# Output projection and embedding gate as 512-column matmuls with high and low parts side by side

## The chip, the cores and the metric

One Trainium2 chip, one core of it. The program is one launch: two transformer layers over 256 tokens. The metric is device time in microseconds (us), from runs of the same program; lower is better. The profile is one more execution with the hardware profiler on. TensorE is called PE, its weight loads PEld, VectorE DVE, ScalarE ACT, GpSimd POOL, and SyncE, which issues the big DMAs, SP.

## The reference

Two layers of a trunk, width 1024, 256 tokens, 32-bit floats. In each layer the normalised state is projected, three mixers (differential attention "da", a state space mixer "ssd", gated linear attention "gla", 512 channels each) run on the projections, and then come the parts that matter here:

```python
mix = jnp.concatenate([y_da, y_ssd.astype(y_da.dtype), y_gla.astype(y_da.dtype)], axis=-1)
h = h + mix @ w_out[i]
f = rms_norm(h, ffn_norm[i])
h = h + (jax.nn.silu(f @ w_ffn_gate[i]) * (f @ w_ffn_up[i])) @ w_ffn_down[i]
h = h + jax.nn.sigmoid(h @ ple_w_gate[i]) * (p[i] @ ple_w_proj[i])
```

`mix @ w_out` is the output projection (1536 to 1024), `h @ ple_w_gate` the embedding gate (1024 to 1024).

## The kernel before

**Products in three parts.** Every 32-bit operand is split in a high part and a low part, and a product is high x high + high x low + low x high. An activation block is one tile of 128 channels x 512: columns 0 to 255 hold the high part of the 256 tokens, columns 256 to 511 the low part. `product_t` with weights as the stationary operand knows two forms. The narrow one (L242 to L245) issues for each 128-channel step k three matmuls of 256 columns, each with a weight load of its own: high weight x high activation (L243), high weight x low activation (L244), low weight x high activation (L245). The wide one (L235 to L239) issues two: high weight x the whole 512 columns (L237), low weight x the 256 high columns (L239), and takes two k at a time (two L237, then two L239). A narrow result is 128x256 and two blocks of output channels share a PSUM bank; a wide result fills a bank of 512 columns, whose two halves have to be added afterwards. The feed-forward uses the wide form; the output projection and the gate use the narrow one.

**Stages.** The work of a layer is a list of units, one per block of weights: projections with the mixers' steps between them, four units `w_o1` (`first`, the ssd and gla channels of `mix`, 8 steps k), two units `w_o2` (`second`, the da channels, 4 steps k, two pairs of output blocks each), 22 units `w_f`, 16 units `w_d`, four units `w_g` (`gate`). After each unit the weights of the second next are loaded (`load_w`): one DMA of 1 MB into one of 3 stage buffers `st`, then for each half of the unit ACT writes the high part `wh` (L212) and DVE the low part `wl` (L213, which reads `wh`). `wh` and `wl` have 6 buffers each, so an L212 can start only when PE has read the half unit six halves earlier to its end.

**The ends of the stages.** Results of the output projection are added to the state `h` on DVE (L934 in `first`, L943 in `second`). `operand` then makes the next activation block from `h`: ACT the high part (L273), DVE the low part (L274). `square` (ACT L283, POOL L286) sums squares for the norm. The first `w_f` unit is issued with `split=6`: steps k 0 to 5 of both output blocks, then k 6 and 7, the blocks that are made last. The da channels of `mix` come from `parts` (ACT L387, DVE L388), one pair for each of four channel blocks and each of two halves of the tokens; four of them read one PSUM tile `pm`. Between `w_d` and `gate`, DVE L1000 updates `h`, and ACT L269 and DVE L270 make the block.

**Order.** A scheduler places the instructions of all engines at build time from its own estimate of when data is there; each engine then runs its list strictly in that order. There are 5 PSUM banks `acc` for these products, used in turn.

Of the kernel before, what the change touches and what calls it, by code (L numbers as in the profile page):

```python
# [16 lines left out]
ALU = mybir.AluOpType  # L17
# [3 lines left out]
P = 128  # L21
D = 1024
T = 256
# [22 lines left out]
O_FFN = O_ATTN + 8  # L46
# [61 lines left out]
def trunk_kernel(ctx: ExitStack, tc: tile.TileContext, a: dict):  # L108
    nc = tc.nc
    pe, dve, act, pool = nc.tensor, nc.vector, nc.scalar, nc.gpsimd  # L110
# [13 lines left out]
    def slot(s, dt=F32):  # L124
        return sp.tile([P, SLOT], dt, tag="slot", name=nm(s))
# [4 lines left out]
    def bank_acc():  # L130
        return ps.tile([P, 512], F32, tag="acc", bufs=NACC, name=nm("acc"))
# [4 lines left out]
    def v3(ap, n):  # L136
        return ap.rearrange("p (a b) -> p a b", a=n)


    par = [cp.tile([P, NPAR], F32, name=f"par{i}") for i in range(DEPTH)]  # L140
    cst = cp.tile([P, NCST], F32, name="cst")
    pos = cp.tile([P, 2, a["pos"].shape[-1]], I32, name="pos")
    h = cp.tile([P, KD, T], F32, name="h")
# [85 lines left out]
    def product_t(out, w, lo, x, ks, n, wide):  # L229


        if wide:

            pairs = list(zip(ks, w, strict=True))
            for p0 in range(0, len(pairs), 2):  # L235
                for k, (wh, _) in pairs[p0:p0 + 2]:
                    pe.matmul(out, wh[:, lo:lo + P], x[k], start=k == 0, stop=False)  # L237
                for k, (_, wl) in pairs[p0:p0 + 2]:
                    pe.matmul(out[:, :T], wl[:, lo:lo + P], x[k][:, :T], start=False, stop=k == n - 1)  # L239
            return  # L240
        for k, (wh, wl) in zip(ks, w, strict=True):
            sh, sl, hi = wh[:, lo:lo + P], wl[:, lo:lo + P], x[k][:, :T]  # L242
            pe.matmul(out, sh, hi, start=k == 0, stop=False)  # L243
            pe.matmul(out, sh, x[k][:, T:], start=False, stop=False)  # L244
            pe.matmul(out[:, :T], sl, hi, start=False, stop=k == n - 1)  # L245

    def gemm_t(blocks, x, wide=False, split=0, apart=False):


        n = len(x)  # L250
        apart = apart or split or wide
        pbs = [bank_acc() for _ in range(2)] if apart else [bank_acc()]
        outs = [pb if wide else pb[:, :T] for pb in pbs] if apart else [pbs[0][:, :T], pbs[0][:, T:]]
        for k0, k1 in ((0, split), (split, n)) if split else ((0, n),):
            for c in range(2):
                w, lo = blocks(c)
                product_t(outs[c], w[k0:k1], lo, x, range(k0, k1), n, wide)
        return [(outs[c], c, c + 1) for c in range(2)] if apart else [(pbs[0], 0, 2)]
# [5 lines left out]
    def operand(x, c, gains):  # L264

        xc = slot("x", F32R)
        hi, lo = xc[:, :T], xc[:, T:]
        if gains is None:
            act.activation(hi, h[:, c], AF.Copy)  # L269
            dve.tensor_tensor(lo, h[:, c], hi.bitcast(F32), ALU.subtract)  # L270
        else:
            g = gains[:, c:c + 1]
            act.activation(hi, h[:, c], AF.Copy, scale=g)  # L273
            dve.scalar_tensor_tensor(lo, h[:, c], g, hi.bitcast(F32), ALU.mult, ALU.subtract)  # L274
        x.append(xc)

    def both(out, pb):
        act.activation(out, pb[:, T:], AF.Copy)
        dve.tensor_tensor(out, pb[:, :T], out, ALU.add)

    def square(c2, acc):
        sq = slot("ssq") if acc is None else slot("sq")
        act.activation(sq, h[:, 2 * c2:2 * c2 + 2].rearrange("p a b -> p (a b)"), AF.Square)  # L283
        if acc is None:
            return sq
        pool.tensor_tensor(acc, acc, sq, ALU.add)  # L286
        return acc
# [514 lines left out]
    def step(S, *names):  # L802
        for n in names:
            if n not in S["gens"]:
                S["gens"][n] = {"da": da_gen, "ssd": ssd_gen, "gates": gla_gates_gen, "gla": gla_gen}[n](S["i"], S)
            next(S["gens"][n], None)
# [119 lines left out]
    def out_units(i, S, x):  # L926

        def first(c2):
            def go(w):
                if c2 < 4:  # L930
                    step(S, *PLAN_OUT[c2])
                pb = gemm_t(lambda c: (w, c * P), S["mix"][1] + S["mix"][2])[0][0]
                hv = h[:, 2 * c2:2 * c2 + 2]
                dve.tensor_tensor(hv, v3(pb, 2), hv, ALU.add)  # L934
            return go

        def second(c4):
            def go(w):
                for c2 in (2 * c4, 2 * c4 + 1):
                    for pb, lo, hi in gemm_t(lambda c: (w, (2 * (c2 % 2) + c) * P), S["mix"][0],  # L940
                                             apart=c2 == 3):
                        hv = h[:, 2 * c2 + lo:2 * c2 + hi]
                        dve.tensor_tensor(hv, v3(pb, hi - lo), hv, ALU.add)  # L943
                        for c in range(2 * c2 + lo, 2 * c2 + hi):
                            operand(x, c, par[i][:, O_FFN:O_FFN + 8])
                    S["acc"] = square(c2, S["acc"])
            return go

        for c2 in range(4):
            units.append((a["w_o1"][i, c2], KD, T, first(c2)))  # L950
        for c4 in range(2):
            units.append((a["w_o2"][i, c4], 4, 512, second(c4)))

    def ffn_units(i, S, x, xg):
# [3 lines left out]
        def summed(pieces):  # L958
            gu = slot("gu")
            for pb, c, _ in pieces:  # L960
                both(gu[:, c * T:(c + 1) * T], pb)
            return gu
# [27 lines left out]
        def down(n):  # L990
            def go(w):
                c, half = n // 2, n % 2
                if half == 0:
                    S["pd"] = bank_acc()
                product_t(S["pd"], w, 0, ax, range(11 * half, 11 * half + 11), NFF, True)
                if half:
                    d = slot("down")[:, :T]
                    both(d, S["pd"])
                    dve.tensor_tensor(d, d, S["rbc"][:, 0], ALU.mult)
                    dve.tensor_tensor(h[:, c], d, h[:, c], ALU.add)  # L1000
                    operand(xg, c, None)
            return go
# [6 lines left out]
    def gate_units(i, S, xg, nxt):  # L1009
        def gate(c2):  # L1010
            def go(w):
                pieces = gemm_t(lambda c: (w, c * P), xg, split=6 if c2 == 0 else 0, apart=c2 == 3)
                g = slot("gate")
                for pb, lo, hi in pieces:
                    s = slice(lo * T, hi * T)
                    gv, hv = v3(g[:, s], hi - lo), h[:, 2 * c2 + lo:2 * c2 + hi]
                    act.activation(g[:, s], pb, AF.Sigmoid)
                    dve.tensor_tensor(g[:, s], g[:, s], S["ple"][c2][:, s], ALU.mult)
                    dve.tensor_tensor(hv, hv, gv, ALU.add)
                    if nxt is not None:  # L1020
                        for c in range(2 * c2 + lo, 2 * c2 + hi):
                            operand(nxt[1], c, par[i + 1][:, O_ATTN:O_ATTN + 8])
                    else:
                        nc.sync.dma_start(a["out"][:, 2 * c2 + lo:2 * c2 + hi], hv)
                if nxt is not None:
                    nxt[0]["acc"] = square(c2, nxt[0]["acc"])
            return go

        for c2 in range(4):
            units.append((a["w_g"][i, c2], KD, T, gate(c2)))  # L1030
# [3 lines left out]
    for i in range(DEPTH):  # L1034
        S = state[i]
        xf, xg = [], []
# [138 lines left out]
```

## Time and profile before

| what | value |
|---|---|
| median of 3 runs | 809.76 us (808.99 to 810.79) |
| profiled execution, its own time | 808.72 us |
| its span in the profile | 806.7 us |
| PE busy | 796.1 us, 99% of the span |
| DVE busy | 624.6 us, 77% |
| ACT busy | 472.8 us, 59% |
| mean granted clock of PE | 0.991 |

The span runs from the first to the last instruction that the profiler saw; the execution's own time has 2.0 us more around it. A matmul's row shows the time from start to its modelled end, which overlaps with the next; what a matmul costs in a dense stretch is read from the distance between starts. The other engines' rows show real lengths, though an instruction may start before the one ahead has ended.

### The profile page before, as it was taken

How to read it: one execution, taken by the hardware profiler on the slowest of the kernel's cores; microseconds unless marked ns; L12 is line 12 of the kernel's file. 1: busy time of each engine (PE TensorE's matmuls, PEld its weight loads, DVE VectorE, ACT ScalarE, POOL GpSimd, SP SyncE). 2: the span in 40 equal slices, each digit the busy share in tenths (PEclk: the TensorE clock that was granted, in tenths of full speed). 3: DMA queues.
4: the chain of work that ended last, by engine and by line, in shares of the span. 5: the costliest groups of instructions: out<-in, count | busy, mean ns of one | idle time of the engine just before them, and what ended most of it. 6: DMA issues, size and time to landing. Idle time of an engine off the chain costs nothing.

```text
span 806.7 us, 13118 instructions
## 1 busy us (share of the span) xinstructions
PE 796.1 (99%) x5026; PEld 703.7 (87%) x5026; DVE 624.6 (77%) x1279; ACT 472.8 (59%) x820; POOL 22.8 (3%) x34
## 2 busy tenths in 40 slices
PE   8999999999999999999999999999999999999997
PEld 6998876899888888888999987778998888888897
DVE  5998977788787777667789699777888777766673
ACT  7767556556665555455667675284566566555461
POOL 2000000002000000000010000000020000000000
PEclk9999989999999999999999999899999999999999
DMA  8764331444655544557554532333445555445541
GB/s 295 278 213 140 139 103 54 157 157 158 209 164 203 188 162 144 179 182 247 207 206 163 177 112 99 107 135 124 158 160 198 197 180 206 138 153 191 196 157 53
DMA packets 24013, 134.92 MB, mean 167 GB/s; under 512 B 2960, under 2 KB 4752, under 8 KB 11408
## 3 DMA queue, kind: packets, MB, share of 16 engines
q1 hardware_dynamic: 23616, 133.57, 48.3%
q8 instruction: 39, 0.64, 0.3%
q0 software_dynamic: 192, 0.52, 0.2%
q14 instruction: 22, 0.18, 0.1%
q10 hardware_dynamic: 144, 0.01, 0.0%
HBM read 133.05 MB, written 1.05 MB: 166 GB/s over the span
## 4 chain that ended last, share of the span: by engine, by line
PE 91%; DVE 3%; ACT 2%; DMA 2%; issue 1%; SPq 0%; DVEq 0%; ACTq 0%
PE acc L237 30%; PE acc L239 15%; PE acc L245 7%; PE acc L244 7%; PE acc L243 7%; PE acc L824 4%; PE acc L825 4%; PE acc L826 4%; PE pm L458 2%; PE pm L602 1%; DMA h<-in_x 1%; PE acc L226 1%; PE acc L225 1%; PE acc L227 1%; DVE wl L213 1%
## 5 line engine op out<-in xcount | busy, mean ns | idle before, releaser
L212 ACT ACTIVATE wh<-st 128x1024 fp32r<-128x1024 f32 (+5 forms) x274 | 267.4, 979 | 234.6 <-PE acc L237 91.3
L213 DVE TENSOR_TENSOR wl<-st,wh 128x1024 fp32r<-128x1024 f32 (+5 forms) x274 | 309.3, 1132 | 105.1 <-ACT wh L212 104.8
L237 PE MATMUL acc<-x,wh 128*128 128x512 f32 x704 | 222.0, 396 | 0.1
L239 PEld LDWEIGHTS acc<-x,wl 128*128 128x128 f32 x704 | 132.3, 188 | 31.2
L239 PE MATMUL acc<-x,wl 128*128 128x256 f32 x704 | 138.4, 278 | 0.0
L237 PE MATMUL acc<-act,wh 128*128 128x512 f32 x352 | 111.8, 395 | 0.0
L237 PEld LDWEIGHTS acc<-x,wh 128*128 128x128 f32 x704 | 107.3, 189 | 0.7 <-DVE x L274 0.7
L245 PE MATMUL acc<-x,wl 128*128 128x256 f32 x320 | 90.7, 283 | 0.9 <-DVE wl L213 0.9
L243 PE MATMUL acc<-x,wh 128*128 128x256 f32 x320 | 90.9, 284 | 0.0
L244 PE MATMUL acc<-x,wh 128*128 128x256 f32 x320 | 90.5, 283 | 0.0
L239 PEld LDWEIGHTS acc<-act,wl 128*128 128x128 f32 x352 | 66.2, 188 | 14.3
L239 PE MATMUL acc<-act,wl 128*128 128x256 f32 x352 | 72.0, 279 | 0.0
L824 PE MATMUL acc<-wh,x 128*128 128x512 f32 x160 | 66.3, 417 | 0.5 <-ACT wh L212 0.5
L825 PE MATMUL acc<-wl,x 128*128 128x512 f32 x160 | 65.1, 407 | 0.0
L826 PE MATMUL acc<-wh,x 128*128 128x512 f32 x160 | 64.4, 403 | 0.0
L245 PEld LDWEIGHTS acc<-x,wl 128*128 128x128 f32 x320 | 61.2, 191 | 1.1 <-DVE wl L213 1.1
L243 PEld LDWEIGHTS acc<-x,wh 128*128 128x128 f32 x320 | 61.2, 191 | 0.2
L244 PEld LDWEIGHTS acc<-x,wh 128*128 128x128 f32 x320 | 61.2, 191 | 0.1
L237 PEld LDWEIGHTS acc<-act,wh 128*128 128x128 f32 x352 | 54.9, 189 | 1.3
L244 PE MATMUL acc<-mix,wh 128*128 128x256 f32 x192 | 54.6, 285 | 0.0
L243 PE MATMUL acc<-mix,wh 128*128 128x256 f32 x192 | 54.3, 286 | 0.0
L245 PE MATMUL acc<-mix,wl 128*128 128x256 f32 x192 | 54.1, 283 | 0.0
(259 smaller groups left out, 1167.8 us busy)
## 6 DMA issues: line engine op xcount, KB each, us to landing
st<-in_w_f SPq DMA_DIRECT2D x44, 1024.0 KB, 4.9
st<-in_w_d SPq DMA_DIRECT2D x32, 704.0 KB, 4.1
st<-in_w_x SPq DMA_DIRECT2D x18, 1024.0 KB, 4.9
st<-in_w_o SPq DMA_DIRECT2D x12, 1024.0 KB, 4.9
st<-in_w_t SPq DMA_DIRECT2D x11, 1024.0 KB, 4.9
st<-in_w_g SPq DMA_DIRECT2D x8, 1024.0 KB, 5.0
st<-in_w_z SPq DMA_DIRECT2D x3, 1088.0 KB, 5.0
st<-in_w_x SPq DMA_DIRECT2D x8, 256.0 KB, 4.8
```

The source lines that it names most:

```text
L212: i_hi = act.activation(wh[:, s], st[:, o], AF.Copy)
L213: i_lo = dve.tensor_tensor(wl[:, s], st[:, o], wh[:, s].bitcast(F32), ALU.subtract)
L225: pe.matmul(out, sh, mh, start=i == 0, stop=False)
L237: pe.matmul(out, wh[:, lo:lo + P], x[k], start=k == 0, stop=False)
L239: pe.matmul(out[:, :T], wl[:, lo:lo + P], x[k][:, :T], start=False, stop=k == n - 1)
L243: pe.matmul(out, sh, hi, start=k == 0, stop=False)
L244: pe.matmul(out, sh, x[k][:, T:], start=False, stop=False)
L245: pe.matmul(out[:, :T], sl, hi, start=False, stop=k == n - 1)
L458: pe.matmul(pb[c][:, j * nk:(j + 1) * nk], q[r, o + qb * P:o + (qb + 1) * P], k[r, o:o + nk], start=True, stop=False)
L824: pe.matmul(pb[b], xh, wh, start=kk_ == 0, stop=False)
L825: pe.matmul(pb[b], xh, wl, start=False, stop=False)
L826: pe.matmul(pb[b], xl, wh, start=False, stop=kk_ == KD - 1)
```

## The change

The output projection and three of the four gate units go to the wide form. `gemm_t` is called with `wide` set, and so takes one bank for each 128-channel output block. In `first` and `second` the new helper `add_both` adds the bank's two halves to `h` one after the other, two DVE instructions of 256 columns (at L283 of the changed file). In the gate, `both` (an ACT copy of one half, a DVE add of the other) first makes the sum in the gate's tile, and the sigmoid reads that tile. The last gate unit (`c2 == 3`) stays narrow.

```diff
+    def add_both(out, pb):
+        for o in (0, T):
+            dve.tensor_tensor(out, pb[:, o:o + T], out, ALU.add)
...
-                pb = gemm_t(lambda c: (w, c * P), S["mix"][1] + S["mix"][2])[0][0]
-                hv = h[:, 2 * c2:2 * c2 + 2]
-                dve.tensor_tensor(hv, v3(pb, 2), hv, ALU.add)
+                for pb, c, _ in gemm_t(lambda c: (w, c * P), S["mix"][1] + S["mix"][2], True):
+                    add_both(h[:, 2 * c2 + c], pb)
...
-                    for pb, lo, hi in gemm_t(lambda c: (w, (2 * (c2 % 2) + c) * P), S["mix"][0],
-                                             apart=c2 == 3):
-                        hv = h[:, 2 * c2 + lo:2 * c2 + hi]
-                        dve.tensor_tensor(hv, v3(pb, hi - lo), hv, ALU.add)
-                        for c in range(2 * c2 + lo, 2 * c2 + hi):
-                            operand(x, c, par[i][:, O_FFN:O_FFN + 8])
+                    for pb, lo, _ in gemm_t(lambda c: (w, (2 * (c2 % 2) + c) * P), S["mix"][0], True):
+                        add_both(h[:, 2 * c2 + lo], pb)
+                        operand(x, 2 * c2 + lo, par[i][:, O_FFN:O_FFN + 8])
...
-                pieces = gemm_t(lambda c: (w, c * P), xg, split=6 if c2 == 0 else 0, apart=c2 == 3)
+                wide = c2 < 3
+                pieces = gemm_t(lambda c: (w, c * P), xg, wide, 6 if c2 == 0 else 0, apart=True)
...
+                    if wide:
+                        both(g[:, s], pb)
+                        pb = g[:, s]
                     act.activation(g[:, s], pb, AF.Sigmoid)
```

The scheduler places the instructions anew around these edits, in both layers in the same way. Below, line numbers of the changed file are 4 higher from L280 on (L387 becomes L391, L388 L392), and a name's number tells tiles of one name apart.

On PE, in layer 0 at the start of `second` (`mix_2089` to `mix_2092` are the da blocks k 0 to 3, `wh_2075` the high weights of k 0 and 1), the kernel before goes through one output pair after the other:

```order
L243 MATMUL acc_2174<-mix_2089,wh_2075 128x256
L244 MATMUL acc_2174<-mix_2089,wh_2075 128x256
L245 MATMUL acc_2174<-mix_2089,wl_2076 128x256
L243 MATMUL acc_2174<-mix_2090,wh_2075 128x256
L244 MATMUL acc_2174<-mix_2090,wh_2075 128x256
L245 MATMUL acc_2174<-mix_2090,wl_2076 128x256
L243 MATMUL acc_2174<-mix_2091,wh_2080 128x256
```

In the changed kernel the da blocks are `mix_2053` to `mix_2056`, and the rows at the same place, after the four output blocks 2126, 2127, 2156 and 2157 have taken k 0 in turn and then k 1 in turn, are:

```order
L239 MATMUL acc_2157<-mix_2054,wl_2040 128x256
L237 MATMUL acc_2126<-mix_2055,wh_2044 128x512
L237 MATMUL acc_2127<-mix_2055,wh_2044 128x512
L237 MATMUL acc_2156<-mix_2055,wh_2044 128x512
L237 MATMUL acc_2157<-mix_2055,wh_2044 128x512
L237 MATMUL acc_2197<-mix_2053,wh_2117 128x512
L237 MATMUL acc_2197<-mix_2054,wh_2117 128x512
L239 MATMUL acc_2197<-mix_2053,wl_2118 128x256
L239 MATMUL acc_2197<-mix_2054,wl_2118 128x256
L237 MATMUL acc_2197<-mix_2055,wh_2122 128x512
L237 MATMUL acc_2126<-mix_2056,wh_2044 128x512
L239 MATMUL acc_2126<-mix_2055,wl_2045 128x256
```

The first four output blocks now advance together, k by k, with the fifth started in between, and so the four end close together instead of one pair after the other.

On ACT, in layer 0 just ahead of that place, the kernel before makes all eight high parts of the da blocks (`pm_2084` is the first half of the tokens, `pm_2101` the second), and then the weights of the first `w_f` unit:

```order
L387 ACTIVATE mix_2089<-pm_2084,gsub 128x128
L387 ACTIVATE mix_2089<-pm_2101,gsub 128x128
L387 ACTIVATE mix_2090<-pm_2084,gsub 128x128
L387 ACTIVATE mix_2090<-pm_2101,gsub 128x128
L387 ACTIVATE mix_2091<-pm_2084,gsub 128x128
L387 ACTIVATE mix_2091<-pm_2101,gsub 128x128
L387 ACTIVATE mix_2092<-pm_2084,gsub 128x128
L387 ACTIVATE mix_2092<-pm_2101,gsub 128x128
L212 ACTIVATE wh_2244<-st_2243 128x1024
L212 ACTIVATE wh_2249<-st_2243 128x1024
```

The changed kernel (`pm_2048` and `pm_2065` are the two halves of the tokens, `st_2187` and `st_2259` the first and second `w_f` unit) has there:

```order
L391 ACTIVATE mix_2055<-pm_2048,gsub 128x128
L212 ACTIVATE wh_2188<-st_2187 128x1024
L391 ACTIVATE mix_2056<-pm_2048,gsub 128x128
L391 ACTIVATE mix_2054<-pm_2065,gsub 128x128
L212 ACTIVATE wh_2193<-st_2187 128x1024
L391 ACTIVATE mix_2055<-pm_2065,gsub 128x128
L212 ACTIVATE wh_2260<-st_2259 128x1024
L391 ACTIVATE mix_2056<-pm_2065,gsub 128x128
L212 ACTIVATE wh_2265<-st_2259 128x1024
L273 ACTIVATE x_2146<-h,par_70 128x256
L273 ACTIVATE x_2151<-h,par_70 128x256
```

Three weight conversions moved ahead of the last mixer parts, and a fourth ahead of the first block of the feed-forward. DVE has its counterparts in the same places: the L213 of `wh_2188` (`wl_2189`) stands between the low parts of `mix_2055` and `mix_2056` of the first half, the L213 of `wh_2260` (`wl_2261`) right ahead of the low part of `mix_2056` of the second half.

On DVE, in layer 0 at the end of the output projection, the kernel before has (`x_2315` and `x_2319` are the blocks k 6 and 7 of the feed-forward, `wl_2395` is weights):

```order
L943 TENSOR_TENSOR h<-acc_2253,h 128x512
L943 TENSOR_TENSOR h<-acc_2288,h 128x256
L274 SCALAR_TENSOR_TENSOR x_2279<-h,par_70,x_2279 128x256
L274 SCALAR_TENSOR_TENSOR x_2282<-h,par_70,x_2282 128x256
L943 TENSOR_TENSOR h<-acc_2289,h 128x256
L274 SCALAR_TENSOR_TENSOR x_2315<-h,par_70,x_2315 128x256
L213 TENSOR_TENSOR wl_2395<-st_2393,wh_2394 128x1024
L274 SCALAR_TENSOR_TENSOR x_2319<-h,par_70,x_2319 128x256
```

The changed kernel has there (`x_2248` and `x_2253` are k 6 and 7; ten adds of the earlier blocks and the blocks k 0 to 3 stand ahead of this piece):

```order
L283 TENSOR_TENSOR h<-acc_2198,h 128x256
L283 TENSOR_TENSOR h<-acc_2228,h 128x256
L283 TENSOR_TENSOR h<-acc_2198,h 128x256
L274 SCALAR_TENSOR_TENSOR x_2217<-h,par_70,x_2217 128x256
L283 TENSOR_TENSOR h<-acc_2228,h 128x256
L283 TENSOR_TENSOR h<-acc_2229,h 128x256
L274 SCALAR_TENSOR_TENSOR x_2222<-h,par_70,x_2222 128x256
L283 TENSOR_TENSOR h<-acc_2229,h 128x256
L213 TENSOR_TENSOR wl_2266<-st_2259,wh_2265 128x1024
L274 SCALAR_TENSOR_TENSOR x_2248<-h,par_70,x_2248 128x256
L274 SCALAR_TENSOR_TENSOR x_2253<-h,par_70,x_2253 128x256
```

The weights' L213 now stands ahead of both last blocks, and 16 adds and 8 blocks are in one row from the first finished output block on.

At the start of the gate, ACT had before (`x_4140` is the last block, k 7):

```order
L278 ACTIVATE down_4135<-acc_4080 128x256
L269 ACTIVATE x_4140<-h 128x256
L212 ACTIVATE wh_4291<-st_4290 128x1024
```

and has now, with the weights of the last gate unit one place earlier (on DVE the L213 of `wh_4205` moves ahead of the low part of k 7 in the same way, L270):

```order
L278 ACTIVATE down_4069<-acc_4014 128x256
L212 ACTIVATE wh_4205<-st_4204 128x1024
L269 ACTIVATE x_4074<-h 128x256
```

PE there pulls the first four steps k of the second gate unit in between k 6 and k 7 of the first.

## Rows read from the trace of the kernel before

**Rows 1.** The page: span, busy time, granted clock by slice, chain that ended last.

```profile
span 806.7 us, 13118 instructions
PE 796.1 (99%) x5026; PEld 703.7 (87%) x5026; DVE 624.6 (77%) x1279; ACT 472.8 (59%) x820; POOL 22.8 (3%) x34
...
PE 91%; DVE 3%; ACT 2%; DMA 2%; issue 1%; SPq 0%; DVEq 0%; ACTq 0%
```

**Rows 2.** Stretches: length, busy PE, PEld, DVE, ACT, POOL; then clock.

```profile
158.40:203.60 45.20, 44.83 (x360) 43.62 (x359) 39.04 (x79) 27.56 (x46) 5.19 (x3) 1.00 0.41 141
158.40:197.70 39.30, 38.96 (x328) 38.73 (x327) 33.20 (x73) 23.32 (x40) 2.30 (x1) 1.00 0.41 138
...
554.80:594.00 39.20, 38.86 (x327) 38.63 (x326) 33.12 (x72) 23.22 (x40) 2.27 (x1) 1.00 0.42 138
```

**Rows 3.** PE's timeline, narrow, then wide: start, length, line, operation.

```profile
187.13 0.28 PE L245 MATMUL acc<-mix,wl 128*128 128x256 f32 x1
...
197.57 0.28 PE L245 MATMUL acc<-mix,wl 128*128 128x256 f32 x1
197.69 0.63 PE L237 MATMUL acc<-x,wh 128*128 128x512 f32 x2
198.16 0.39 PE L239 MATMUL acc<-x,wl 128*128 128x256 f32 x2
...
209.59 0.63 PE L237 MATMUL acc<-x,wh 128*128 128x512 f32 x2
...
213.77 0.63 PE L237 MATMUL acc<-x,wh 128*128 128x512 f32 x2
```

**Rows 4.** PE's timeline, last steps k of the first feed-forward unit, layer 0.

```profile
201.87 0.93 PE L237 MATMUL acc<-x,wh 128*128 128x512 f32 x2
202.64 0.40 PE L239 MATMUL acc<-x,wl 128*128 128x256 f32 x2
```

**Rows 5.** DVE's timeline, layer 0, output projection to feed-forward (idle time before, releaser).

```profile
180.47 0.68 DVE L934 TENSOR_TENSOR h<-acc,h 128x512 f32<-128x512 f32 x1
181.07 0.60 DVE L388 SCALAR_TENSOR_TENSOR mix<-pm,gsub,mix 128x128 fp32r<-128x128 f32 x2
...
190.52 0.89 DVE L274 SCALAR_TENSOR_TENSOR x<-h,par,x 128x256 fp32r<-128x256 f32 x2 [0.58 <-ACT x L273]
...
199.59 1.21 DVE L213 TENSOR_TENSOR wl<-st,wh 128x1024 fp32r<-128x1024 f32 x1
200.73 1.52 DVE L274 SCALAR_TENSOR_TENSOR x<-h,par,x 128x256 fp32r<-128x256 f32 x1
```

**Rows 6.** POOL's timeline, same place.

```profile
200.36 1.60 POOL L286 TENSOR_TENSOR ssq<-ssq,sq 128x512 f32<-128x512 f32 x1 [0.98 <-ACT sq L283]
```

**Rows 7.** DVE's timeline in the feed-forward: two independent 256-column instructions in a row.

```profile
231.80 0.42 DVE L971 TENSOR_TENSOR act<-gu,act 128x256 fp32r<-128x256 f32 x1
232.14 0.42 DVE L279 TENSOR_TENSOR gu<-acc,gu 128x256 f32<-128x256 f32 x1
```

**Rows 8.** ACT's timeline, layer 0, around the last mixer parts and the next weights.

```profile
181.44 0.63 ACT L387 ACTIVATE mix<-pm,gsub 128x128 fp32r<-128x128 f32 x2 [0.18 <-DVE mix L388]
...
184.86 1.06 ACT L212 ACTIVATE wh<-st 128x1024 fp32r<-128x1024 f32 x1 [0.35 <-PE acc L244]
...
198.26 1.04 ACT L212 ACTIVATE wh<-st 128x1024 fp32r<-128x1024 f32 x1
199.21 0.49 ACT L273 ACTIVATE x<-h,par 128x256 fp32r<-128x256 f32 x1
```

**Rows 9.** PE and DVE at the gate's start, layer 0.

```profile
382.83 0.28 PE L239 MATMUL acc<-act,wl 128*128 128x256 f32 x1
...
387.15 0.43 DVE L270 TENSOR_TENSOR x<-h,x 128x256 fp32r<-128x256 f32 x1 [0.48 <-ACT x L269]
```

**Rows 10.** DVE at the end of layer 0's gate.

```profile
406.38 1.43 DVE L1018 TENSOR_TENSOR gate<-gate,ple 128x256 f32<-128x256 f32 x1 [0.30 <-ACT gate L1017]
```

## Prediction

> **What bounds the kernel now.** I read the page first: PE is busy 99% of the span and holds 91% of the chain that ended last [rows 1]. So a stage is as long as its stream of matmuls, and other engines cost time only where PE waits for them. Next come the stretches of the stages touched [rows 2]. From 158.40 to 203.60, the output projection of layer 0 and the first feed-forward unit, DVE is busy 39.04 of 45.20 us, far above its 77% over the span; layer 1 repeats the same numbers within 0.1 us, so all that follows counts twice. The granted clock in these stretches is 1.00, the 2.4 GHz level, in which PE had been working all the time. Last the timelines. PE's gives the price of both forms and the one wait at the stage's end [rows 3, 4]; those of DVE, ACT and POOL give the durations of what feeds it [rows 5 to 8].
>
> **What PE gains.** In the narrow form 87 matmuls lie between the starts 187.13 and 197.57 [rows 3]: 0.1200 each, 0.360 for the three of one step k. In the wide form six groups of four (two k each) lie between 209.59 and 213.77: 0.697 a group, 0.348 for a step. The two wide ones take 0.47 of a group (197.69 to 198.16). The change turns 64 + 32 + 48 = 144 steps per layer, 288 in all: 288 x 0.0117 = 3.4 us gained, if PE never waits. Its size is fixed by rows of the same two shapes. The Trainium skill, page "TensorE: Matmul & The Clock Gate", section "Back-to-back issue gap", has N/2.4 + 2.5 ns for a matmul of N columns when warm. By that a narrow step is 327.5 and a wide one 325 ns, and an estimate of the gain is 288 x 2.5 ns = 0.7 us. The rows show 360 and 348, so I go by them; the page's rule is a rival below.
>
> **What DVE and ACT pay.** Two independent 256-column instructions start 0.34 apart [rows 7]; a 512-column add takes 0.60 before the next (180.47 to 181.07, [rows 5]). In each layer seven adds of 512 (4.2 us) and two of 256 (0.7 us) become 32 of 256 (10.9 us): 6.0 us more for DVE in a stretch where it has 45.20 - 39.04 = 6.2 us free, and PE wants to be 1.1 us quicker there. That only works if DVE never waits. It does wait, because the order was made anew and both engines run their lists strictly. I follow the lists of the changed kernel by hand, with layer 0's times; 0.1 is taken for a signal between engines. Unit prices: L212 0.95 until the next on ACT [rows 8]; L213 1.14 (199.59 to 200.73), L388 0.26 until the next and 0.34 to its end, L274 0.40 and 0.49 [rows 5]; L387 0.36 to its end and 0.27 until the next (two in 0.63, [rows 8]).
>
> *First wait, k 1 of `second`.* With 0.19 us less per unit, PE ends `first` at 185.5 instead of 186.2 (the 96 narrow matmuls of `second`, 11.5 us, before 197.69, [rows 3]); a wait for the last `L497` transposes (0.1 at most, since their DVE chain now has twelve adds in it, before two) is in that. It runs k 0 of four blocks (0.94) and wants `mix_2054` complete at 186.4. That needs ACT's high part of the second half, which stands behind the L212 of `wh_2188`. This L212 takes the buffers of the last `first` unit's k 0 to 3, which PE has read four steps (1.4 us) before that end, by 184.1: it runs 184.2 to 185.2. Two mixer parts bring ACT to 185.8. DVE first does that L213 (185.4 to 186.5), then two L388: 187.1. PE waits 0.7.
>
> *Second wait, k 3.* From 187.2 PE takes 4 x 0.465 for k 1, 4 x 0.235 for k 2, and five matmuls of the fifth block (0.93): it wants `mix_2056` at 190.9. ACT's L212 of `wh_2260` stands ahead of that part, and its buffers are free only when PE has done k 0 and 1 of all four blocks, 189.0: 189.2 to 190.1, the part to 190.5. On DVE the L213 of that weight stands ahead as well: 190.3 to 191.4, L388 to 191.8. PE waits 0.9. In the kernel before both waits are absent: all eight pairs L387/L388 come ahead of the weights, and L212 waits for PE, not PE for it (0.35 before 184.86, [rows 8]).
>
> *Third wait, k 6 and 7 of the feed-forward.* The four blocks now end together, 192.3 to 193.7, and PE ends the projection at 191.85 + 5 x 0.465 + 12 x 0.348 = 198.35 (before 197.7). From 192.5 DVE has 16 adds, 8 L274 and an L213 ahead of k 7: 5.4 + 3.2 + 1.1 = 9.8 us without a gap, so 202.3 at the earliest. Two gaps come on top. ACT's first block stands behind the L212 of `wh_2265`, whose buffers PE frees at 193.7, so it is there at 195.4 and not 195.0. And L213 and L274 stop while POOL adds squares: the L274 of 200.73 took 1.52 instead of 0.49 and ended at 202.25, 0.29 after POOL's at 201.96 [rows 5, 6]. In the new order POOL's add falls at 201.3 to 202.5, on the L213: k 6 is there at 204.0, k 7 at 204.45. PE, with 26 matmuls ahead (12 x 0.348 + 0.47), wants k 6 at 203.0: it waits 1.2. Before, the pair of L237 at 201.87 gave way to L239 only at 202.64, 0.77 later where 0.47 is normal: a wait of 0.3 [rows 3, 4]. Net 0.9.
>
> So a layer pays 0.1 + 0.7 + 0.9 + 0.9 = 2.6 us, both together 5.3. Bounds: each wait can be 0, if what hides it is quicker than my hand trace; and each 0.7 more, half an L213 and a bit, if one more weight gets in between. For the sum that is 0 to 9.5.
>
> *Gate.* k 7 was ready at 387.58 [rows 9]. Now the L212 of the last gate unit stands ahead, and waits for PE to read k 0 to 3 of both blocks of the first: 382.95 + 20 x 0.174 = 386.4. With L212, L213 (to 388.7) and L270 it is there at 389.1. PE has 12 steps of the first unit, two wide matmuls of k 6 and four steps of the second unit ahead, 16 x 0.348 + 0.47 = 6.05 us from 382.95, and wants it at 389.0. A wait of 0.1 to 0.4; I take 0.25 per layer, 0.5. The six ACT copies, adds and sigmoids of the wide gate units lie beside 5.6 us of matmuls each and cost nothing by themselves. But they come on top of DVE's and ACT's list: its unit has two L213, two adds, two products, two adds to `h`, two L274, 2.3 + 0.7 + 0.7 + 0.7 + 0.8 = 5.2 of 5.6 us. It runs late, and the blocks k 6 and 7 for layer 1 come at about 413.7 to 415, where PE wants k 6 at 413.6. Before, POOL stopped an instruction there too (1.43 instead of 0.42, [rows 10]). I take 0.6, between 0 and 1.3, once. The weights' DMAs move with the L213 that free their stages, by a few us at most, and have more than 10 us until PE needs them. The tail after the last matmul is as before, since the last gate unit stays narrow.
>
> **Sum.** -3.4 + 5.3 + 0.5 + 0.6 = +3.0 us, against the profiled execution's 808.72 us: 811.7. The median of the runs shown is 809.76, 1.04 above that execution; for the median I forecast 809.8 + 3.0 = 812.8.
>
> **Rivals.** *Forecast: PE waits for the new order.* 812.8, own range 811.4 to 815.5; for it: DVE's 6.0 us into 6.2 free. Chance 0.65.
> *The mixer parts come in time, only the crowd before the feed-forward stays.* If ACT and DVE run about 1 us ahead of my trace at 185, both waits in `second` are gone: 812.8 - 2 x 1.7 = 809.4. For it: the kernel before was done with these parts at 184.9, over 1 us before use. Against: three L212 and their L213 now stand between them. Chance 0.18.
> *Everything hides.* DVE fills its 6.2 us, blocks arrive when wanted, and the gain stays: 809.8 - 3.4 + 0.5 = 806.9. This decides if the waits of a layer are together under 1.0 us. Against: the third wait is there already before. Chance 0.13.
> *The narrow form is not dearer by itself.* A wide step in these stages would then cost as much less as the matmul's columns say, nearly nothing, with the same waits: 812.8 + 2.7 = 815.5. Against: 0.348 in rows of the same shape. Chance 0.04. (This is the page's rule, "Back-to-back issue gap"; the trace does not bear it out.)
>
> **Numbers.** What this measurement can tell from no change is 0.2%, 1.6 us. Faster (under 808.1): 0.13. Within: 0.18. Slower (over 811.4): 0.69. The range 808.5 to 815.5 takes in the second case whole and leaves out most of the third and the far end of the waits.
>
> **What would show it.** In the profile after: the distance of narrow starts gone from the projection, wide groups 0.697 apart; gaps on PE of 0.7 and 0.9 about 28 and 32 us after the projection's start, with DVE's low part of a mixer tile as the releaser; about 1.2 before k 6 of the first feed-forward unit; the projection's stretch no shorter than 39.3 us; DVE busy over 90% of it. If the stretch is about 38.2 us and the gap before k 6 is 0.3, the third case holds. I would be wrong above all if ACT reaches the last mixer parts sooner than PE frees the weights' buffers in my trace.

## The result

The changed kernel takes 813.77 us, the kernel before 807.87 us in runs beside it (medians of 20 runs each): a ratio of 1.0064, 95% interval 1.0046 to 1.0082. By that ratio it is slower by about 5.2 us (the medians lie 5.9 apart); 3.0 were forecast.

One thing is needed to read the profiles. The granted clock falls in some executions and not in others, in stretches that the change doesn't touch (last section): the profiled execution of before has two such falls and a mean granted clock of 0.991, that of after has none and 0.999, so their spans, 806.7 and 806.3 us, say nothing about the change. What compares are lengths of stages. The page of the changed kernel, span, busy time and chain:

```profile
span 806.3 us, 12636 instructions
...
PE 789.8 (98%) x4738; PEld 681.6 (85%) x4738; DVE 639.4 (79%) x1345; ACT 477.4 (59%) x836; POOL 22.1 (3%) x34
...
PE 86%; DVE 7%; ACT 3%; DMA 2%; issue 1%; SPq 0%; ACTq 0%; DVEq 0%
```

Beside [rows 1], PE is busy for 6 us less (a part of that is the full clock, not less work), and its share of the chain fell from 91 to 86%, while DVE's rose from 3 to 7%: PE now waits for DVE. The view of PE's waits says where (total, times, longest):

```profile
PE acc L237 <- DVE x L274: 3.1, 2, 1.5
PE acc L237 <- DVE mix L392: 2.1, 4, 0.6
...
PE acc L830 <- DVE x L274: 0.5, 1, 0.5
```

None of the three exists in the kernel before. PE's timeline of layer 0 shows the first two in place, the gate's start and the boundary to layer 1 behind them (start, length, ..., count; in brackets the idle time and its releaser):

```profile
155.90 0.71 PE L237 MATMUL acc<-mix,wh 128*128 128x512 f32 x2
...
182.92 1.09 PE L237 MATMUL acc<-mix,wh 128*128 128x512 f32 x4
184.44 0.50 PE L237 MATMUL acc<-mix,wh 128*128 128x512 f32 x1 [0.42 <-DVE mix L392]
184.78 0.40 PE L239 MATMUL acc<-mix,wl 128*128 128x256 f32 x2
...
188.04 0.39 PE L237 MATMUL acc<-mix,wh 128*128 128x512 f32 x1
189.08 0.50 PE L237 MATMUL acc<-mix,wh 128*128 128x512 f32 x1 [0.65 <-DVE mix L392]
189.42 0.40 PE L239 MATMUL acc<-mix,wl 128*128 128x256 f32 x2
...
195.73 0.62 PE L237 MATMUL acc<-x,wh 128*128 128x512 f32 x2
...
200.17 0.63 PE L237 MATMUL acc<-x,wh 128*128 128x512 f32 x2
202.34 0.90 PE L237 MATMUL acc<-x,wh 128*128 128x512 f32 x2 [1.54 <-DVE x L274]
203.08 0.40 PE L239 MATMUL acc<-x,wl 128*128 128x256 f32 x2
...
388.75 0.39 PE L239 MATMUL acc<-x,wl 128*128 128x256 f32 x2
389.17 0.50 PE L237 MATMUL acc<-x,wh 128*128 128x512 f32 x1
...
414.17 0.39 PE L829 MATMUL acc<-wl,x 128*128 128x512 f32 x1
415.02 0.50 PE L830 MATMUL acc<-wh,x 128*128 128x512 f32 x1 [0.46 <-DVE x L274]
```

A wait is read between starts: four wide matmuls take 0.93, so after 182.92 the next belonged at 183.85 and came at 184.44, and that one held PE for 0.34 where 0.235 is usual: 0.69 lost. At 189.08 it is 0.91 in the same way. The pair at 200.17 should have been followed 0.47 later and was 2.17 later, and its successor took 0.74: 1.97 lost. Another 0.26 goes in small delays ahead of it: the 26 matmuls between 195.73 and the end of that pair, 200.64, take 4.91 us, and 4.65 by the rows' prices. DVE and POOL behind the last wait, from their timelines:

```profile
198.62 2.27 DVE L213 TENSOR_TENSOR wl<-st,wh 128x1024 fp32r<-128x1024 f32 x1
200.81 1.87 DVE L274 SCALAR_TENSOR_TENSOR x<-h,par,x 128x256 fp32r<-128x256 f32 x2
```

```profile
198.52 3.49 POOL L290 TENSOR_TENSOR ssq<-ssq,sq 128x512 f32<-128x512 f32 x2 [2.22 <-ACT sq L287]
```

Where [rows 5] has an L213 of 1.21 us, here it takes 2.27, and two L274 (0.9 together otherwise) take 1.87. POOL now has two adds in a row there, 198.52 to 202.01, over just these instructions. The kernel before has the same two adds, but apart: that of [rows 6] and one ahead of it, and each stopped one L274 (this one 1.28 us, that of 200.73 in [rows 5] 1.52, where 0.48 is usual):

```profile
198.09 1.29 POOL L286 TENSOR_TENSOR ssq<-ssq,sq 128x512 f32<-128x512 f32 x1 [1.04 <-ACT sq L283]
```

```profile
198.39 1.28 DVE L274 SCALAR_TENSOR_TENSOR x<-h,par,x 128x256 fp32r<-128x256 f32 x1
```

Layer 1 of the changed kernel has the same rows as its layer 0, to a few hundredths.

So that runs can be compared whatever their clock elsewhere, I take distances between first starts on PE: P, first matmul of the projection; F, first of the feed-forward; G, first of the gate; N, the norm's matmuls of layer 1; E, the last matmul. In these stretches the granted clock was 1.00, except where said. Where nothing in it was changed, the same stage repeats to 0.04 us from layer to layer and build to build.

| kernel | P to F | F to G, layers 0 / 1 | G to N | G to E | sum, both layers | change | ratio (95%) |
|---|---|---|---|---|---|---|---|
| before | 39.23 | 185.26 / 185.26 | 33.92 | 22.92 | 505.82 | | |
| changed | 39.83 | 187.23 / 187.21 | 34.53 | 22.65 | 511.28 | +5.46 | 1.0064 (1.0046 to 1.0082) |
| gate_only | 39.25 | 185.26 / 185.25 | 34.50 | 22.65 | 506.17 | +0.35 | 1.0007 (0.9983 to 1.0031) |
| proj_only | 39.86 | 187.21 / 187.24 | 33.92 | 22.90 | 510.98 | +5.16 | 1.0086 (1.0054 to 1.0117) |
| parts_first | 38.19 | 186.22 / 186.22 | 34.54 | 22.63 | 505.99 | +0.17 | 1.0008 (0.9986 to 1.0030) |
| squares_late | 39.84 | 188.88 / 188.92 | 34.54 | 22.65 | 514.67 | +8.85 | 1.0114 (1.0083 to 1.0145) |
| half_late | 39.83 | 186.79 / 186.79 | 34.51 | 22.65 | 510.41 | +4.59 | 1.0042 (1.0015 to 1.0068) |
| no_pool | 39.83 | 185.22 / 185.22 | 34.50 | 22.67 | 507.24 | +1.42 | 1.0002 (0.9982 to 1.0023) |
| first_gate | 38.75 | 189.51 / 187.96 | 34.50 | 22.65 | 512.12 | +6.30 | 1.0082 (1.0053 to 1.0112) |
| norm_later | 38.15 | 185.57 / 185.57 | 34.51 | 22.65 | 504.60 | -1.22 | 0.9986 (0.9958 to 1.0014) |
| gate_last | 38.18 | 185.57 / 185.55 | 33.93 | 22.68 | 504.10 | -1.72 | 0.9970 (0.9944 to 0.9996) |
| before_norm | 39.24 | 185.27 / 185.27 | 33.92 | 22.89 | 505.84 | +0.02 | 1.0020 (0.9996 to 1.0044) |

The sum's 5.46 us for the change agree with the ratio (5.2 us). The stage sums that the expectations name run on to the span's end, 4.4 to 4.7 us more (510.35 before, 515.72 changed).

### The profile page after: what moved, and what is told of

It is laid out like the page before. It is cut to its first block, busy times and chain, and to the rows that moved or that the text cites. A ratio compares the mean times of both kernels' runs of the same rounds, so it can differ in the third digit from the quotient of the medians.

```text
span 806.3 us, 12636 instructions
## 1 busy us (share of the span) xinstructions
PE 789.8 (98%) x4738; PEld 681.6 (85%) x4738; DVE 639.4 (79%) x1345; ACT 477.4 (59%) x836; POOL 22.1 (3%) x34
## 4 chain that ended last, share of the span: by engine, by line
PE 86%; DVE 7%; ACT 3%; DMA 2%; issue 1%; SPq 0%; ACTq 0%; DVEq 0%
PE acc L237 37%; PE acc L239 18%; PE acc L828 3%; PE acc L830 3%; PE acc L829 3%; PE acc L245 3%; PE acc L244 3%; PE acc L243 3%; DVE wl L213 3%; PE pm L462 2%; ACT wh L212 2%; DMA st<-in_w_x 1%; PE acc L226 1%; PE acc L227 1%; PE acc L225 1%
## 5 line engine op out<-in xcount | busy, mean ns | idle before, releaser
L212 ACT ACTIVATE wh<-st 128x1024 fp32r<-128x1024 f32 (+5 forms) x274 | 267.8, 979 | 244.3 <-PE acc L237 110.6
L213 DVE TENSOR_TENSOR wl<-st,wh 128x1024 fp32r<-128x1024 f32 (+5 forms) x274 | 310.1, 1134 | 103.6 <-ACT wh L212 102.9
L237 PE MATMUL acc<-x,wh 128*128 128x512 f32 x800 | 252.6, 397 | 3.1 <-DVE x L274 3.1
L239 PE MATMUL acc<-x,wl 128*128 128x256 f32 x800 | 157.5, 278 | 0.0
L237 PEld LDWEIGHTS acc<-x,wh 128*128 128x128 f32 x800 | 122.5, 189 | 5.6 <-DVE x L274 4.8
L828 PE MATMUL acc<-wh,x 128*128 128x512 f32 x160 | 65.0, 408 | 0.8 <-ACT wh L212 0.8
L237 PE MATMUL acc<-mix,wh 128*128 128x512 f32 x192 | 63.0, 403 | 2.1 <-DVE mix L392 2.1
L245 PE MATMUL acc<-x,wl 128*128 128x256 f32 x224 | 63.5, 283 | 0.9 <-DVE wl L213 0.9
L830 PE MATMUL acc<-wh,x 128*128 128x512 f32 x160 | 63.5, 397 | 0.5 <-DVE x L274 0.5
L243 PE MATMUL acc<-x,wh 128*128 128x256 f32 x224 | 63.7, 284 | 0.0
L244 PE MATMUL acc<-x,wh 128*128 128x256 f32 x224 | 63.4, 283 | 0.0
L244 PEld LDWEIGHTS acc<-x,wh 128*128 128x128 f32 x224 | 43.0, 192 | 0.1
L243 PEld LDWEIGHTS acc<-x,wh 128*128 128x128 f32 x224 | 42.9, 192 | 0.1
L239 PEld LDWEIGHTS acc<-mix,wl 128*128 128x128 f32 x192 | 35.8, 188 | 7.1
L279 DVE TENSOR_TENSOR gu<-acc,gu 128x256 f32<-128x256 f32 x88 | 36.7, 417 | 2.9 <-ACT gu L278 2.9
```

The source lines that it names most:

```text
L212: i_hi = act.activation(wh[:, s], st[:, o], AF.Copy)
L213: i_lo = dve.tensor_tensor(wl[:, s], st[:, o], wh[:, s].bitcast(F32), ALU.subtract)
L828: pe.matmul(pb[b], xh, wh, start=kk_ == 0, stop=False)
L830: pe.matmul(pb[b], xl, wh, start=False, stop=kk_ == KD - 1)
```

## Experiments

The theory (A): the wide form saves what its rows say, and the loss is PE's waits at the stages' ends, which the new order of ACT, DVE and POOL brings. The rivals: the wide form saves nothing here (B), or DVE's 6 us more a layer are the bound, in whatever order (C).

**One half of the change each** (gate_only: `first` and `second` as before; proj_only: `gate` as before). Against the changed kernel, the first three lines are of gate_only, which puts back `second` in the same way, and the last is of proj_only.

```diff
-                for pb, c, _ in gemm_t(lambda c: (w, c * P), S["mix"][1] + S["mix"][2], True):
-                    add_both(h[:, 2 * c2 + c], pb)
+                pb = gemm_t(lambda c: (w, c * P), S["mix"][1] + S["mix"][2])[0][0]
...
-                wide = c2 < 3
...
```

> Only the gate is wide, the output projection as before. Theory A (the loss is made of waits at the ends of the stages, which the new order brings; the wide form itself saves 0.0117 us a step): the gate saves 0.56 us a layer less 0.3 for its k 7, and the boundary to layer 1 costs 0.85 once: +0.3 us, ratio 1.000 (0.998 to 1.002). Rival B (the wide form saves nothing in these stages): +1.4 us, 1.002. If the gate held most of the loss it would be 1.004 or more.

> Only the output projection is wide, the gate as before. Theory A: the 2.5 us a layer between the projection's start and the norm's matmuls stay, +5.1 us, ratio 1.006. Rival (the loss comes from the gate and the layer's boundary): 1.001 to 1.002.

The halves add up: +0.35 and +5.16 against +5.46 together. The projection is the loss. The gate alone gives 0.24 to 0.27 us a layer and pays 0.85 at the boundary. Both fit A; for the gate alone, B would be +1.4.

**Weights behind the mixer parts** (parts_first). `parts` notes its two instructions, and the conversions of units 25 and 26, the first two `w_f`, go behind the last of them; the work is that of the changed kernel.

```diff
+        last_parts[:] = [i_hi.ins, i_lo.ins]
...
+    FFN_AT = (25, 26)
...
+                if n % (len(units) // DEPTH) in FFN_AT:
+                    for ins in last_parts:
+                        es.enter_context(tc.issue_after(ins))
```

> All as changed, but the weights of the first two feed-forward units are converted behind the last mixer parts on ACT and DVE, as in the kernel before. Theory A, each wait by itself: the waits at k 1 and k 3 of the second part of the projection (0.69 and 0.91 us a layer) go, -3.2 us, ratio 1.0025. Rival C (DVE's 6 us more are the bound of the whole stretch, and what is not waited for at k 1 and k 3 is waited for at k 6): PE's waits at k 1 and k 3 go too, but the one at k 6 grows from 2.0 by about 1.6 us, ratio 1.006 as for the changed kernel.

P to F falls from 39.83 to 38.19, under before by 1.04: 96 steps give 0.0108 us each, so the wide form saves nearly what the rows say (B and the rival of the formula are out), and both waits in `second` are gone. What none of the expectations had: the wait at k 6 goes too. The new binding changed more than the weights' places: the first L274 comes 31.8 us after the projection's start, as in the kernel before (32.1, changed 36.7), so the output blocks end one after the other again, and POOL's adds fall apart (starts 194.70, 196.75, 201.06). C is out: DVE has the same amount of work. One new wait of 0.89 us a layer appears, at the norm, whose sum stands on DVE behind an L213 that takes 2.30 us beside the add of 201.06:

```profile
202.72 0.40 PE L239 MATMUL acc<-x,wl 128*128 128x256 f32 x2
204.00 0.61 PE L298 MATMUL pm<-ones,ssq 128*128 128x1 f32 x4 [0.89 <-DVE ssq L295]
```

**What holds k 6: three tries at the same place.** squares_late moves the last two squares of ACT behind the last block, and so POOL's adds; half_late moves the long L213 behind the last two L274; no_pool leaves POOL's last two adds out and keeps every other row of the order. In this sequence, from `second`, `load_w` and `square`:

```diff
+                if c4:
+                    with tc.issue_after(last_block[0]):
+                        for c2 in (2, 3):
+                            S["acc"] = square(c2, S["acc"])
...
+                    if last is not None and k0:
+                        es.enter_context(tc.issue_after(last))
                     i_lo = dve.tensor_tensor(wl[:, s], st[:, o], wh[:, s].bitcast(F32), ALU.subtract)
...
+        if c2 < 2 or not part:
             pool.tensor_tensor(acc, acc, sq, ALU.add)
```

> All as changed, but the last two squares of the norm (ACT) stand behind the last block's high part, so that POOL's two adds come after the last blocks. Theory A with POOL's part in it: the L213 that took 2.27 us takes about 1.15 and the two L274 that took 1.87 take 0.9; the wait at k 6 falls from 2.0 to about 0.3 us, -1.5 us a layer, ratio 1.003, if the norm's matmuls don't wait for the later sum in its place. Rival C (DVE's amount of work alone): the wait stays, ratio 1.006.

> As changed, but the low weights of the second half of the second feed-forward unit (the L213 of 2.27 us) stand behind the low parts of the last two blocks on DVE. If the L213 itself is what stands in the way of k 6: the wait at k 6 falls from 2.0 to under 0.5 us, -1.5 us a layer, the stages touched 512.7 us, 1.0045. If it is POOL's two adds that stop DVE, they stop the two low parts now: k 6 and 7 come when POOL is done, as before, the wait stays at 1.5 to 2.0 us, 515.2, 1.0095 at most.

> As changed, but POOL's last two square sums ahead of the feed-forward are left out (the norm then lacks the squares of the last four channel blocks); the order on all other engines stays the same row by row. If POOL is what stops DVE there: the L213 of 2.27 us takes 1.2 and the two L274 of 1.87 take 0.9, k 6 is there 2 us earlier, PE's wait falls from 2.0 to at most 0.3 us; from the projection's start to the gate 225.3 instead of 227.05 us in both layers, -3.4 us together, ratio about 1.002. Rival C (the row of adds and blocks on DVE alone): nothing changes, 227.05 and 1.006.

no_pool settles it. Its DVE and PE at the place:

```profile
199.25 1.22 DVE L213 TENSOR_TENSOR wl<-st,wh 128x1024 fp32r<-128x1024 f32 x1
200.39 0.88 DVE L274 SCALAR_TENSOR_TENSOR x<-h,par,x 128x256 fp32r<-128x256 f32 x2
```

```profile
200.82 1.08 PE L237 MATMUL acc<-x,wh 128*128 128x512 f32 x4
201.74 0.40 PE L239 MATMUL acc<-x,wl 128*128 128x256 f32 x2
```

With the order unchanged and only POOL quiet, L213 is back from 2.27 to 1.22, the L274 from 1.87 to 0.88, PE runs from k 5 into k 6 without a gap, and F to G is 185.22: 2.0 us under the changed kernel, so much do POOL's two adds cost a layer, and 0.04 under before. The 16 adds and 8 blocks in one row do not make PE wait at k 6 by themselves. What they leave are small delays ahead of it, 0.28 us (the 26 matmuls from 196.36 end at 201.29), about as much as the kernel before lost at its own k 6 (0.3 in the prediction). half_late agrees: the two L274, now ahead, are stopped in the L213's place, by the same adds (lines are 3 to 5 higher here).

```profile
198.53 2.70 DVE L278 SCALAR_TENSOR_TENSOR x<-h,par,x 128x256 fp32r<-128x256 f32 x2
```

```profile
198.24 2.71 POOL L295 TENSOR_TENSOR ssq<-ssq,sq 128x512 f32<-128x512 f32 x2 [2.22 <-ACT sq L292]
```

Its sum, 514.81 to the span's end, is nearly that of the expectation's second branch (515.2, where 512.7 was the first). Neither branch held whole: PE sits idle for 0.92 us at k 6, between the two (under 0.5, and 1.5 to 2.0), since the L213's 1.2 us no longer come first, and the ratio, 1.0042, is that of the first. F to G falls by only 0.44. squares_late also frees k 6 (PE's rows are dense up to 203.7), and pays more for it: the adds then run beside an L213 that takes 2.32 us, and PE waits for the norm's sum and goes on at half the clock. So its expectation held for the wait at k 6, but the condition in its last clause, that the norm's matmuls don't wait, was not met, and the time went up (lines here are 1 or 2 higher):

```profile
201.71 3.68 POOL L292 TENSOR_TENSOR ssq<-ssq,sq 128x512 f32<-128x512 f32 x2 [4.02 <-ACT sq L289]
```

```profile
205.90 0.61 PE L300 MATMUL pm<-ones,ssq 128*128 128x1 f32 x4 [1.83 <-DVE ssq L297]
...
207.18 1.05 PE L238 MATMUL acc<-x,wh 128*128 128x512 f32 x2
...
208.46 1.05 PE L238 MATMUL acc<-x,wh 128*128 128x512 f32 x2
```

**Only the long part wide** (first_gate: `second` as before, all else as changed).

```diff
-                    for pb, lo, _ in gemm_t(lambda c: (w, (2 * (c2 % 2) + c) * P), S["mix"][0], True):
+                    for pb, lo, hi in gemm_t(lambda c: (w, (2 * (c2 % 2) + c) * P), S["mix"][0],
+                                             apart=c2 == 3):
...
```

> The first part of the projection (8 steps of each of 8 output blocks) and the gate wide, the second part (the da channels) narrow as before. Theory A (the waits belong to the four wide blocks of the second part that end together): the gain of 64 steps a layer stays, -1.5 us, with the gate's +0.3: the stages touched take 509.2 us, ratio 0.9985. Rival C (DVE's added amount is the bound): 16 adds of 256 for 4 of 512 are 3.0 us more a layer on DVE, and the wait at k 6 grows by 1 us or more: 511 or above, 1.001 or above.

Here my theory, as I had it then, fell: I had put the waits down to the four wide blocks of `second`. They are narrow here, the waits in `second` are gone (38.75), and yet PE loses more ahead of the feed-forward's last blocks than in the changed kernel (1.78 and 0.68 us idle in each layer, 2.7 from F to G in layer 1; layer 0 lost 1.55 more, with the clock at its lower level). The time alone is what C expected, but the rows show another cause, two adds of POOL in a row over the last four blocks:

```profile
198.56 3.70 DVE L274 SCALAR_TENSOR_TENSOR x<-h,par,x 128x256 fp32r<-128x256 f32 x4
```

```profile
198.45 2.73 POOL L290 TENSOR_TENSOR ssq<-ssq,sq 128x512 f32<-128x512 f32 x2 [2.49 <-ACT sq L287]
```

(Two L274 take 0.88 without POOL.) By these rows what decides is whether POOL's adds meet the last blocks, not the form of `second`. This kernel was not run with POOL quiet, so here the cause is read and not tested.

**Clearing the rest** (norm_later: parts_first, with the norm's matmuls one unit later; gate_last: in addition the gate wide in layer 1 alone; before_norm: the kernel before with the later norm alone).

```diff
-                if j == 0:
+                if j == 1:
                     S["rcol"] = token_norm(S["acc"])
...
-                wide = c2 < 3
+                wide = nxt is None and c2 < 3
```

> As the run that converts the weights behind the mixer parts, and in addition the norm's sum and its matmuls are asked for after the second feed-forward unit and not after the first. Theory A (what is left of the loss there is PE waiting 0.9 us a layer for POOL's last square sum): the stages touched go from 510.47 to 508.7 us, 1.6 under before, ratio 0.998. Rival: the later sum makes the scaling rows late for the third unit, and the wait only moves: 510.4, 1.000.

> As the run with the later norm, and the gate wide only in the second layer, narrow in the first. Theory A (the gate pays only where no next layer's blocks wait behind it): the 0.6 us of the boundary go, the stages touched take 508.1 us, 2.2 under before, ratio 0.997. Rival (the gate in layer 0 saves as much as in layer 1): no better than the run with the later norm, 0.998 or above.

> The kernel before with the norm's sum asked for after the second feed-forward unit, nothing else: a control for the two runs that have the later norm. If their gain over before comes from the wide form alone, this one gains nothing (0 to -0.3 us, ratio 0.9995 to 1.0005), since PE does not wait at the norm in the kernel before. If the later norm is a gain by itself, -0.5 us a layer or more, 0.999 or below.

The later norm takes 1.39 us off parts_first (1.8 were there to take; 0.2 a layer is now waited for the rows made from the sum) and nothing off the kernel before (+0.02), so this is the wide form's gain coming through. gate_last takes the boundary's 0.6 away (G to N 33.93): -1.72 us in the stages where -2.2 were expected, ratio 0.997 with an interval that ends just below 1, a little faster than the kernel before. In it, PE between the projection's start and the gate of layer 0 waits in two places, 0.2 us each:

```profile
PE pm L798 <- DVE fyn L790: 0.2, 1, 0.2
PE pm L309 <- DVE rcol L192: 0.2, 1, 0.2
```

## Why the prediction was right, and where its size was off

The direction held, and so did the mechanism (PE waits for the new order) and the places of the waits; the time came out at 813.8 for 812.8. That it lies so near is luck: the kernel before took 807.9 in the runs beside it, not 809.8, and the loss was 5.2 to 5.5 us, not 3.0. Two errors of some 2 us, one in the start and one in the loss, nearly cancel. Step by step, in us:

| step of the prediction | forecast | measured |
|---|---|---|
| PE's gain, 288 steps | -3.4 | -3.1 (0.0108 a step, from the 96 of a projection in parts_first) |
| first wait, k 1, a layer | 0.7 | 0.69 |
| second wait, k 3, a layer | 0.9 | 0.91 |
| third wait, k 6 and 7, net, a layer | 0.9 | 1.97 (F to G) |
| last transposes in `first`, a layer | 0.1 | no wait in the rows |
| k 7 of the gate, a layer | 0.25 | 0.29 (0.18 idle, 0.11 restart) |
| boundary to layer 1, once | 0.6 | 0.85 |

**The gain.** Groups are 0.697 apart as before; where four blocks take turns, one wide and two narrow matmuls take 0.48 where 0.465 is usual. The formula weighed there (the Trainium skill, "TensorE: Matmul & The Clock Gate", "Back-to-back issue gap") would give 0.0025 a step. The page states it for a single matmul by itself and says that it counts wrong in a stream; these steps stand in a stream, and parts_first measures 0.0108, near the rows' 0.0117.

**The first two waits** came where and as long as the hand trace had them, closer than the 0.1 us that it took for a signal. What released them is what it named:

```profile
182.63 1.23 DVE L213 TENSOR_TENSOR wl<-st,wh 128x1024 fp32r<-128x1024 f32 x1 [0.74 <-ACT wh L212]
183.78 0.60 DVE L392 SCALAR_TENSOR_TENSOR mix<-pm,gsub,mix 128x128 fp32r<-128x128 f32 x2
...
187.54 1.23 DVE L213 TENSOR_TENSOR wl<-st,wh 128x1024 fp32r<-128x1024 f32 x1 [1.10 <-ACT wh L212]
188.68 0.34 DVE L392 SCALAR_TENSOR_TENSOR mix<-pm,gsub,mix 128x128 fp32r<-128x128 f32 x1
```

A weight's L213 stands ahead of the mixer part for which PE waits, and DVE sat idle (0.74 and 1.10) before it, for ACT's L212: not short of time, but in the wrong order. parts_first, which changes the order alone, takes both away.

**The third wait is the step that was mis-sized**, by 1.1 us a layer, 2.1 of the 2.5 missing. The hand trace had one add of POOL stopping one L213. It did not follow ACT's last two squares, which feed these adds. They start 1.40 apart now, in the kernel before 2.26 (197.34 and 199.60 on ACT), and an add takes 1.3 and more, so the two adds join: 3.49 us in a row. In that row POOL seems to wait too, for the L213 between its adds: in half_late the same two take 2.71.

```profile
197.76 0.62 ACT L287 ACTIVATE sq<-h 128x512 f32<-128x512 f32 x1
...
199.16 0.62 ACT L287 ACTIVATE sq<-h 128x512 f32<-128x512 f32 x1
```

By the prediction's own sum the row of 16 adds, 8 blocks and an L213 was done at 202.3, before PE wanted k 6 at 203.0, and only what came on top made the wait. no_pool bears that out: without the two adds there is no wait at k 6. The mechanism, DVE stopped for as long as POOL adds, was seen in [rows 5, 6] and stands in the Trainium skill, "SBUF — State Buffer", "SBUF: two separate sides", as an exclusive lock on a shared pair of ports that is held for the whole instruction. The trace agrees: L213 took 2.27 with POOL's adds beside it and 1.22 without. I had counted it for a single add, where POOL's queue needed the same hand trace as ACT's and DVE's.

**DVE's filling** was the reason that I gave first, and it does not bear the weight. For the projection's stretch I had forecast over 90% busy; the changed kernel has 34.84 of 39.83 us, 87%. norm_later, which does the same work, has 35.22 of 38.15, 92%, and there PE waits hardly at all:

```profile
155.90:195.73 39.83, 38.52 (x231) 33.24 (x230) 34.84 (x90) 22.58 (x38) 0.76 (x1) 1.00 0.39 133
```

```profile
156.23:194.38 38.15, 37.91 (x232) 33.28 (x230) 35.22 (x92) 23.35 (x41) 1.29 (x1) 1.00 0.41 134
```

So a fuller DVE went with a shorter stretch than before (39.23). The rival "everything hides", with a chance of 0.13, was a matter of order: with the weights bound behind the mixer parts and the later norm (norm_later), 1.2 of the 3.1 us come through.

**The boundary** was 0.85 for 0.6: 0.62 of it is the gap at 415.02, the rest small delays of the same layer's matmuls. The blocks there (1.91 for two L274) lie beside POOL's add as well:

```profile
414.49 1.91 DVE L274 SCALAR_TENSOR_TENSOR x<-h,par,x 128x256 fp32r<-128x256 f32 x2
```

```profile
414.71 1.41 POOL L290 TENSOR_TENSOR ssq<-ssq,sq 128x512 f32<-128x512 f32 x1 [2.90 <-ACT sq L287]
```

That POOL alone makes this wait was not tried. That gate_last takes it away shows only that the wide gate does.

## What to carry to other kernels

When a change makes one engine's work cheaper by adding to others, list the new order of every engine whose instructions stand ahead of the next block, POOL's few included, before believing a count of free time: here 6 us more a layer on DVE cost almost nothing in a good order, and 5 us over both layers in the one that the scheduler chose. A small stage pays only if nothing is waiting behind its end; mending the ends (weights behind the parts that PE wants first, the norm's sum one unit later, the gate narrow where a next layer follows) turned +0.6% into -0.3%. And a stage's length between two starts on the bound engine repeats to 0.04 us, where whole times scatter by 8.

## What the runs showed of the hardware

The granted clock falls to its lower level (1.2 GHz, 0.50) in places that differ between executions of one program. In the profiled execution of before, around 110 us (windows of 2 us: length, busy PE, PEld, DVE, ACT, POOL, clock):

```profile
110.00:112.00 2.00, 2.00 (x11) 2.00 (x11) 0.47 (x1) 0.00 (x0) 0.00 (x0) 0.50 0.93 393
112.00:114.00 2.00, 2.00 (x7) 1.71 (x7) 1.42 (x3) 0.56 (x3) 0.00 (x0) 0.50 0.00 0
```

PE was busy throughout, and the changed kernel's execution had 1.00 there. Runs of the kernel before at a mean clock of 0.999 and more take 802 to 803 us, at 0.991 about 809; those of the changed kernel take 807.5 to 808.3 at 0.999 and about 813.8 at 0.991, so the loss is 5 us at either. The fall can also follow a wait. In squares_late, in both layers:

```profile
204.00:206.00 2.00, 0.17 (x2) 0.10 (x1) 0.84 (x3) 1.25 (x3) 1.39 (x1) 1.00 0.91 385
206.00:208.00 2.00, 2.00 (x9) 1.73 (x10) 2.00 (x7) 0.00 (x0) 0.00 (x0) 0.65 0.04 8
208.00:210.00 2.00, 2.00 (x8) 1.77 (x7) 1.06 (x2) 0.02 (x1) 0.00 (x0) 0.50 0.99 254
```

PE sat idle for 1.83 us, and within 1 us after it went on, the clock fell: a wide group took 1.28 (207.18 to 208.46) where 0.697 is usual. In first_gate waits of 1.78 and 0.68 us were followed by such a fall in layer 0 (+1.55 us) and not in layer 1, and the 1.54 us of the changed kernel by none, in either layer. So three of six waits of this length were followed by a fall, and the one that can be priced cost 1.55 us more. That the wait brought it is not shown, since the clock also fell with PE busy.
